# A seven-product matmul with three of its four results as one running sum in a PSUM bank

## The chip, the cores and the metric

The kernel runs on one core of a Trainium2 chip. The time is the device time of one execution in microseconds, as a median over runs; a profiled execution gives the span from the first to the last instruction, and the trace behind it. TensorE (PE) multiplies matrices, and its weight loads are listed as PEld; VectorE (DVE) and ScalarE (ACT) work elementwise; GpSimd (POOL) and SyncE (SP) mostly issue loads here.

## The reference

Two decoder layers over a sequence of 256 rows of width 2048, in float32. Per layer, cut to the matmuls that matter here:

```python
h = rmsnorm(x); proj = h @ w_in            # GLU pair, q, k, v, forget logits, two gates
y_conv = conv(...) @ w_conv_out;  y_attn = attention(...) @ w_attn_out
x = x + (sigmoid(g_conv) * y_conv + sigmoid(g_attn) * y_attn) @ w_out
gate, up = split(rmsnorm(x) @ w_gate_up)   # 2 x 5632 columns
x = x + (silu(gate) * up) @ w_down
x = x + sigmoid(rmsnorm(x) @ w_ple_gate) * (p[i] @ w_ple_proj)
```

A final rmsnorm ends it. Nearly all the work is a 256-row operand times a wide weight matrix that is read once.

## The kernel before, in words

**Precision and slabs.** A matmul here works on float32r numbers. To keep float32's precision each operand is split into a high part h and a rest l, and a product is three matmuls: xh wh, xh wl, xl wh (`Sum.add`, lines 181 to 186). A weight slab is a tile `raw` of 128 x 1024 (two k-blocks of 128 by 512 columns, 512 KB). `fetch` (133) loads it through SP's queue into one of 8 `raw` buffers. `split` (138) makes h by a ScalarE copy (line 141, the rounding) and l by a VectorE subtraction (line 142); five buffers each, `wh` and `wl`. Two k-blocks, two blocks of 128 rows and three matmuls make 12 matmuls of 512 columns a plain slab.

**The seven-product form.** `fast_chunks` (238) computes two column chunks of 512, weights w1 and w2, over all of k. Of the k-groups of 512 it takes the first one or two (`fast`) in a form with seven products instead of eight; the rest are plain slabs. For a fast group, A11 and A12 are the halves of w1's slab pair, "A21" = w2's first half and A22 = w2's second half; the operand's four blocks and four of their sums are kept in `Fast` (343), made by `make` (362) as M1, T2, T3, N4X. Each product has 6 matmuls. Results go to seven running sums: `c11`, `c12` and `c21` are parts of the result tiles c1 and c2 in the two-bank PSUM tiles `mm`; `p1`, `q5`, `q6`, `q7` have a bank `ms` each, which is all four of the `ms` banks. Transposes and small matmuls use `ms` banks too.

**Order in a group** (lines 274 to 292). Fetch a11 and sm (w2's first half); POOL's queue adds w1's first half onto sm while it loads (276). Fetch a22 and a12. Products: p1 with a11, c21 with a22, a plain slab (`go`), c11 with a12, usually another plain slab, q7 with sm; then VectorE adds a22 to sm; q6 with it; a11 becomes sm - a11; q5; a12 becomes a12 + sm; c12. The three VectorE sums work in place on raw tiles (helpers in lines 271 and 272).

**Evacuation** (lines 293 to 297, 300, 304). ScalarE copies p1 to `u1`; VectorE takes q6 from it, adds q7, and adds q5 twice: four instructions of 128 x 512 that read a bank. After more plain slabs c1 is added to u1, and c2 minus u2 is the second result. Other work (transposes, attention steps, the depthwise convolution on VectorE) is put between the plain slabs after the evacuation, by the queues `turns`, `tasks` and `background`.

**What sets the order.** Each engine runs its queue in order. The framework that builds the queues follows the program's order as a priority: it may put a later instruction ahead of one whose inputs would not be there yet. Semaphores and buffers are its work too: a load waits until its buffer is free, and a write into a bank waits for readers of what was there.

**Where it is called.** `fast_chunks` runs 48 times: the two gates, the output projection, gate/up, down, and the per-layer embedding gate.

Of the kernel before, what the change touches and what calls it, by code (L numbers as in the profile page):

```python
# [12 lines left out]
AF = mybir.ActivationFunctionType  # L13
ALU = mybir.AluOpType
# [31 lines left out]
def trunk(ctx, tc, xT, xR, pT, wI, wF, wC, wA, wOut, wGU, wD, wPG, wPP, vec, bF, gF, out):  # L46
    nc = tc.nc
# [11 lines left out]
    act, dve, pe = nc.scalar, nc.vector, nc.tensor  # L59
    uid = iter(range(1 << 30))  # L60

    def pair(dtype=F32):
        return pairs.tile([P, 2, 512], dtype, tag="pair", name=f"pair{next(uid)}")
# [20 lines left out]
    def run():  # L84
        for _ in range(len(turns)):
            turns.popleft()()
        if tasks:
            tasks.popleft()()

    def fill(n):  # L90
        credit[0] += n
        while background and credit[0] > 0:
            cost, op = background.popleft()
            credit[0] -= cost
            op()
        if not background:
            credit[0] = 0
# [35 lines left out]
    def fetch(src):  # L133
        raw = raws.tile([P, 2, 512], F32, tag="raw", name=f"raw{next(uid)}")
        nc.sync.dma_start(raw.rearrange("p k n -> p (k n)"), src)
        return raw

    def split(raw):
        h = whs.tile([P, 2, 512], F32R, tag="wh", name=f"wh{next(uid)}")
        l = wls.tile([P, 2, 512], F32R, tag="wl", name=f"wl{next(uid)}")  # L140
        act.activation(h, raw, AF.Copy)  # L141
        dve.tensor_tensor(l, raw, h.bitcast(F32), op=ALU.subtract)  # L142
        recent[0] = h
        return h, l
# [26 lines left out]


    class Sum:
        def __init__(self, n, bank):
            self.n, self.left, self.bank = n, n, bank

        @property
        def t(self):
# [2 lines left out]
        def add(self, xh, xl, wh, wl):  # L181
            start = self.left == self.n
            self.left -= 1
            pe.matmul(self.t, lhsT=xh, rhs=wh, start=start, stop=False)  # L184
            pe.matmul(self.t, lhsT=xh, rhs=wl, start=False, stop=False)  # L185
            pe.matmul(self.t, lhsT=xl, rhs=wh, start=False, stop=self.left == 0)  # L186

    def once(make):

        made = []  # L190

        def get():
            if not made:
                made.append(make())
            return made[0]

        return get

    def sums_of_blocks(n1, n2=None):
        t = once(bank_mm)  # L200
        return t, Sum(n1, lambda: t()[:, 0, :]), Sum(n1 if n2 is None else n2, lambda: t()[:, 1, :])

    def plain(sums, xs, k0, parts, blocks=range(2)):
        h, l = parts
        for kk in range(2):
            for b in blocks:
                xh, xl = xs[k0 + kk]
                sums[b].add(xh(b), xl(b), h[:, kk, :], l[:, kk, :])

    def await_x(xs, ks):  # L210
        while not all(k in xs for k in ks):
            assert turns or tasks
            run()
# [24 lines left out]
    def fast_chunks(fast, w1, w2, xs, ks, first, by_block=None):  # L238

        nf, nk = 2 * len(fast), 4 * len(ks)
        p1, q5, q6, q7 = (Sum(nf, once(bank_ms)) for _ in range(4))
        c1, c11, c12 = sums_of_blocks(nf + nk)
        c2, c21, c22 = sums_of_blocks(nf + nk, nk)
        if by_block is not None:
            c22 = Sum(nk, once(bank_ms))
        left = deque()
        for w, sums in ((w1, (c11, c12)), (w2, (c21, c22))):
            for g, k0 in enumerate(ks):  # L250
                for half in range(2):
                    left.append((w[len(fast) + g][:, half * 1024 : (half + 1) * 1024], sums, k0 + 2 * half))
        state = dict(quiet=True)

        def go(n=1):
            for _ in range(n):
                src, sums, k0 = left.popleft()
                parts = split(fetch(src))
                await_x(xs, (k0, k0 + 1))
                plain(sums, xs, k0, parts)  # L260
                if not state["quiet"]:
                    fill(CONV // 2 + len(left) % 2)
                    run()

        def product(to, operand, raw):
            h, l = split(raw)
            xh, xl = operand
            for kk in range(2):
                to.add(xh(kk), xl(kk), h[:, kk, :], l[:, kk, :])

        add = lambda o, a, b: dve.tensor_tensor(o, a, b, op=ALU.add)  # L271
        sub = lambda o, a, b: dve.tensor_tensor(o, a, b, op=ALU.subtract)  # L272
        u1, u2 = pair(), pair()
        for g, f in enumerate(fast):
            a11, sm = fetch(w1[g][:, :1024]), fetch(w2[g][:, :1024])
            nc.gpsimd.dma_start(sm.rearrange("p k n -> p (k n)"), w1[g][:, :1024], accum_op=ALU.add)
            a22, a12 = fetch(w2[g][:, 1024:]), fetch(w1[g][:, 1024:])
            product(p1, f(B11), a11)
            product(c21, f(N4X), a22)
            go()  # L280
            product(c11, f(B21), a12)
            if len(left) > 2 * len(ks):
                go()
            if nk == 8 and len(fast) == 1:
                run()
            product(q7, f(T3), sm)
            add(sm, sm, a22)
            product(q6, f(T2), sm)
            sub(a11, sm, a11)
            product(q5, f(M1), a11)  # L290
            add(a12, a12, sm)
            product(c12, f(B22), a12)
        act.activation(u1[:, 0, :], p1.t, AF.Copy)
        sub(u1[:, 1, :], u1[:, 0, :], q6.t)
        add(u2[:, 0, :], u1[:, 1, :], q7.t)
        add(u1[:, 1, :], u1[:, 1, :], q5.t)
        add(u2[:, 1, :], u2[:, 0, :], q5.t)
        state["quiet"] = False
        go(len(left) - 2 * len(ks))
        add(u1, u1, c1())  # L300
        first(u1)
        if by_block is None:
            go(len(left))
            sub(u2, c2(), u2)
            return u2
        go(len(left) - 4)
        held = [(split(fetch(src)), k0) for src, _, k0 in left]
        for b, c in enumerate((c21, c22)):
            for parts, k0 in held:
                plain([c, c], xs, k0, parts, [b])  # L310
            sub(u2[:, b, :], c.t, u2[:, b, :])
            by_block(b, u2)
# [25 lines left out]

        return (lambda b: o[:, b * P : (b + 1) * P]), (lambda b: o[:, S + b * P : S + (b + 1) * P])

    B11, B12, B21, B22, M1, T2, T3, N4X = range(8)

    class Fast:

# [17 lines left out]
        def make(self):  # L362
            f = lambda n: self.f[n // 4][:, n % 4]
            sub = lambda o, a, b, op: dve.tensor_tensor(f(o), f(a), f(b), op=op)  # L364
            sub(M1, B11, B12, ALU.subtract)
            sub(T2, M1, B22, ALU.add)
            sub(T3, B22, B12, ALU.subtract)
            sub(N4X, B21, T2, ALU.subtract)
            self.h, self.l = [], []
            for t in self.f:  # L370
                h, l = (pair(F32R).rearrange("p a b -> p (a b)") for _ in range(2))
                t = t.rearrange("p n k s -> p (n k s)")
                act.activation(h, t, AF.Copy)  # L373
                dve.tensor_tensor(l, t, h.bitcast(F32), op=ALU.subtract)  # L374
                self.h.append(h.rearrange("p (n k s) -> p n k s", n=4, k=2))
                self.l.append(l.rearrange("p (n k s) -> p n k s", n=4, k=2))
            self.f = None
# [167 lines left out]
    for i in range(L):  # L545
# [296 lines left out]
        def sigmoids(c, nf):  # L842

            ts = []

            def gate(t):
                for b in range(2):
                    act.activation(t[:, b, :], t[:, b, :], AF.Sigmoid, scale=norm.r(b))
                ts.append(t)

            gate(fast_chunks(norm.fast[:nf], wI[i, c], wI[i, c + 1], norm.xs, range(4 * nf, KD, 4), gate))
            return ts
# [38 lines left out]
        for n in range(0, N4, 2):  # L891
            by = (0, 1, 2, 3) if n == 0 else (0, 3, 1, 2)
            onto_x(norm, n + 1)(
                fast_chunks(
                    [fast_merged[g] for g in by[: 1 + n // 2]], *([wOut[i, m][g] for g in by] for m in (n, n + 1)),
                    merged, [4 * g for g in by[1 + n // 2 :]], onto_x(norm, n),
                )
            )
# [4 lines left out]
        for part, nch in enumerate(FFN_PARTS):  # L903
            hid = {}
            fast_hid = [Fast() for _ in range(nch - 2)]
            for c in range(c0, c0 + nch):
                w1, w2 = wGU[i, 2 * c], wGU[i, 2 * c + 1]
# [12 lines left out]
                else:  # L920
                    nf = 1 if c == c0 else 2
# [9 lines left out]
            for n in range(0, N4, 2):  # L931
                await_x(hid, (4 * c0,))
                on = after if part == len(FFN_PARTS) - 1 else None
                nf = 1 if n == 0 else len(fast_hid)
# [132 lines left out]
```

## Time and profile before

| | |
|---|---|
| median of 3 runs | 2793.24 us (2793.18 to 2793.36) |
| profiled execution | 2793.7 us, span 2791.8 us |
| granted TensorE clock | 0.999 |
| bytes read from HBM | 580.85 MB, 209 GB/s over the span |
| ACT busy | 1660.0 us, 59% |
| POOL busy | 79.4 us, 3% |
| DMA engines | 5 to 7 tenths busy in most slices |

How to read it: a group's row gives the line, the engine, the operation, out<-in by the program's names, shapes, the count, then busy time and the mean of one in ns, and behind the second bar the idle time before it and who ended it. Matmuls are pipelined: a record of 0.39 us overlaps its neighbours, and the distance between two starts is what one costs. In the view by windows a row is a stretch, its length, and then the busy time of each engine with its number of instructions, the clock, the DMA share and GB/s. A timeline row has start, duration, engine, line, operation, tiles, count, and in brackets the idle time before it with its releaser.

### The profile page before, as it was taken

To read this page: it belongs to the slowest core of one execution; us is meant where nothing else is said; L and a number is where in the kernel's file an instruction comes from. 1 tells how busy PE (TensorE), PEld (TensorE's weight loads), DVE (VectorE), ACT (ScalarE), POOL (GpSimd) and SP (SyncE) were. 2 spreads that over 40 slices of the span, in tenths; PEclk is the share of its full clock that TensorE was granted. 3 is DMA by queue.
4 is the path that set the end of the run, shared out by engine and by line. 5 is a ranking of instruction groups with operands and counts; after the bars stand their busy time and mean duration, and the time that the engine had idled before them with its cause. 6 is when DMAs were issued, how large, how long until landed. Compare 5 with 4: busy or idle time off the path is not lost.

```text
span 2791.8 us, 34941 instructions
## 1 busy us (share of the span) xinstructions
PE 2773.9 (99%) x12568; PEld 2293.5 (82%) x12568; DVE 2507.1 (90%) x3003; ACT 1660.0 (59%) x2002; POOL 79.4 (3%) x121
## 2 busy tenths in 40 slices
PE   9999999999999999999999999999999999999998
PEld 7888888888888888888888888888888888888886
DVE  7999889888989988999979988988799899889998
ACT  7445766565556655656754466655665565556565
POOL 0000000000000000000000000000000000000000
PEclk9999999999999999999999999999999999999999
DMA  7555557666676766776655555575666677677674
GB/s 299 188 182 185 199 186 227 198 217 201 217 226 220 227 218 220 224 221 203 215 186 190 185 181 199 189 233 184 228 205 215 216 232 231 203 229 218 217 239 131
DMA packets 161597, 585.24 MB, mean 210 GB/s; under 512 B 18192, under 2 KB 18448, under 8 KB 161168
## 3 DMA queue, kind: packets, MB, share of 16 engines
q1 hardware_dynamic: 149040, 539.50, 56.5%
q0 software_dynamic: 11520, 41.95, 8.3%
q8 instruction: 98, 1.61, 0.2%
q10 hardware_dynamic: 864, 1.57, 0.2%
q14 instruction: 75, 0.61, 0.1%
HBM read 580.85 MB, written 2.10 MB: 209 GB/s over the span
## 4 chain that ended last, share of the span: by engine, by line
PE 93%; DVE 3%; issue 3%; ACT 1%; POOL 0%; POOLq 0%; ACTq 0%; DVEq 0%
PE mm L186 25%; PE mm L185 25%; PE mm L184 25%; PE ms L184 5%; PE ms L185 5%; PE ms L186 5%; PE ms L334 2%; DVE wl L142 1%; DVE raw L271 0%; PE ms L726 0%; ACT wh L141 0%; PE ms L755 0%; DVE pair L374 0%; PE ms L745 0%; DVE pair L271 0%
## 5 line engine op out<-in xcount | busy, mean ns | idle before, releaser
L141 ACT ACTIVATE wh<-raw 128x1024 fp32r<-128x1024 f32 x1254 | 1300.5, 1058 | 1022.7 <-PE mm L186 576.7
L142 DVE TENSOR_TENSOR wl<-raw,wh 128x1024 fp32r<-128x1024 f32 x1254 | 1501.0, 1219 | 212.4 <-ACT wh L141 204.9
L184 PE MATMUL mm<-wh,pair 128*128 128x512 f32 x3224 | 1261.9, 392 | 1.1 <-ACT pair L324 0.7
L185 PE MATMUL mm<-wl,pair 128*128 128x512 f32 x3224 | 1256.6, 390 | 0.9 <-DVE wl L142 0.8
L186 PE MATMUL mm<-wh,pair 128*128 128x512 f32 x3224 | 1256.8, 390 | 0.5 <-DVE pair L325 0.5
L186 PEld LDWEIGHTS mm<-wh,pair 128*128 128x128 f32 x3224 | 605.2, 188 | 128.4 <-DVE pair L325 1.4
L185 PEld LDWEIGHTS mm<-wl,pair 128*128 128x128 f32 x3224 | 605.6, 188 | 126.3 <-DVE wl L142 3.2
L184 PEld LDWEIGHTS mm<-wh,pair 128*128 128x128 f32 x3224 | 605.4, 188 | 126.0 <-ACT pair L324 1.7
L184 PE MATMUL ms<-wh,pair 128*128 128x512 f32 x680 | 265.7, 391 | 0.1
L186 PE MATMUL ms<-wh,pair 128*128 128x512 f32 x680 | 264.7, 389 | 0.0
L185 PE MATMUL ms<-wl,pair 128*128 128x512 f32 x680 | 264.6, 389 | 0.0
L569 DVE SCALAR_TENSOR_TENSOR pair<-pair,vecs,pair 128x256 f32<-128x256 f32 x480 | 201.1, 474 | 0.0
L271 DVE TENSOR_TENSOR raw<-raw,raw 128x1024 f32<-128x1024 f32 x160 | 195.4, 1222 | 2.6
L184 PEld LDWEIGHTS ms<-wh,pair 128*128 128x128 f32 x680 | 127.7, 188 | 28.0 <-ACT pair L998 0.9
L186 PEld LDWEIGHTS ms<-wh,pair 128*128 128x128 f32 x680 | 127.6, 188 | 26.7
L185 PEld LDWEIGHTS ms<-wl,pair 128*128 128x128 f32 x680 | 127.7, 188 | 26.0
L272 DVE TENSOR_TENSOR raw<-raw,raw 128x1024 f32<-128x1024 f32 x80 | 98.0, 1225 | 2.6
L271 DVE TENSOR_TENSOR pair<-pair,ms 128x512 f32<-128x512 f32 x144 | 93.9, 680 | 0.0
L272 DVE TENSOR_TENSOR pair<-mm,pair 128x1024 f32<-128x1024 f32 (+1 forms) x48 | 58.1, 1210 | 11.5 <-PE mm L186 11.4
L271 DVE TENSOR_TENSOR pair<-pair,mm 128x1024 f32<-128x1024 f32 x48 | 58.3, 1215 | 5.5 <-PE mm L186 5.5
L374 DVE TENSOR_TENSOR pair<-pair,pair 128x1024 fp32r<-128x1024 f32 x52 | 62.8, 1217 | 0.0
L373 ACT ACTIVATE pair<-pair 128x1024 fp32r<-128x1024 f32 x52 | 54.3, 1055 | 2.7 <-DVE pair L364 1.6
(168 smaller groups left out, 1065.0 us busy)
## 6 DMA issues: line engine op xcount, KB each, us to landing
raw<-in_wGU_dram SPq DMA_DIRECT2D x352, 512.0 KB, 4.8
raw<-in_wI_dram SPq DMA_DIRECT2D x287, 512.0 KB, 4.0
raw<-in_wD_dram SPq DMA_DIRECT2D x176, 512.0 KB, 4.8
raw<-in_wOut_dram SPq DMA_DIRECT2D x64, 512.0 KB, 4.6
raw<-in_wPG_dram SPq DMA_DIRECT2D x64, 512.0 KB, 4.9
raw<-in_wGU_dram POOLq DMA_DIRECT2D x36, 512.0 KB, 7.9
raw<-in_wA_dram SPq DMA_DIRECT2D x32, 512.0 KB, 4.7
raw<-in_wC_dram SPq DMA_DIRECT2D x32, 512.0 KB, 4.9
```

Of the source, the lines that this page charges most:

```text
L141: act.activation(h, raw, AF.Copy)
L142: dve.tensor_tensor(l, raw, h.bitcast(F32), op=ALU.subtract)
L184: pe.matmul(self.t, lhsT=xh, rhs=wh, start=start, stop=False)
L185: pe.matmul(self.t, lhsT=xh, rhs=wl, start=False, stop=False)
L186: pe.matmul(self.t, lhsT=xl, rhs=wh, start=False, stop=self.left == 0)
L271: add = lambda o, a, b: dve.tensor_tensor(o, a, b, op=ALU.add)
L272: sub = lambda o, a, b: dve.tensor_tensor(o, a, b, op=ALU.subtract)
L334: pe.transpose(pt[:, kk * S + b * P : kk * S + (b + 1) * P], src(b)[:, c : c + P], ident)
L373: act.activation(h, t, AF.Copy)
L374: dve.tensor_tensor(l, t, h.bitcast(F32), op=ALU.subtract)
L569: dve.scalar_tensor_tensor(cv[c], u[c][:, j : j + S], w, cv[c], op0=ALU.mult, op1=ALU.add,)
```

## The change

p1, q6 and q7 become one running sum `chain` in one bank with three stations: after the products with B11 it holds p1; after those with NT2 (the negative of T2) it holds p1 - q6; after those with T3 it holds p1 - q6 + q7. ScalarE copies it at each station. `Sum` gets an argument `rests`, so that the last matmul of each third is marked as an end. The products with a11 of all groups go to the start of the call, those with sm (T3) to its end; sm is fetched first and each later group's sm ahead of the sums of the group before; the sum sm + a22 is put into a22 instead of sm. `u1` and `u2` are taken from their pool later. In `make`, T2 becomes NT2 by one scalar_tensor_tensor instruction.

```diff
     class Sum:
-        def __init__(self, n, bank):
-            self.n, self.left, self.bank = n, n, bank
+        def __init__(self, n, bank, rests=1):
+            self.n, self.left, self.bank, self.rest = n, n, bank, n // rests
...
-            pe.matmul(self.t, lhsT=xl, rhs=wh, start=False, stop=self.left == 0)
+            pe.matmul(self.t, lhsT=xl, rhs=wh, start=False, stop=self.left % self.rest == 0, **kw)
...
-        p1, q5, q6, q7 = (Sum(nf, once(bank_ms)) for _ in range(4))
+        chain, q5 = Sum(3 * nf, once(bank_ms), 3), Sum(nf, once(bank_ms))
...
-        u1, u2 = pair(), pair()
+        def third(g):
+            sm = fetch(w2[g][:, :1024])
+            nc.gpsimd.dma_start(sm.rearrange("p k n -> p (k n)"), w1[g][:, :1024], accum_op=ALU.add)
+            return sm
+
+        s3 = [third(0)]
+        a11s = []
         for g, f in enumerate(fast):
-            a11, sm = fetch(w1[g][:, :1024]), fetch(w2[g][:, :1024])
-            nc.gpsimd.dma_start(sm.rearrange("p k n -> p (k n)"), w1[g][:, :1024], accum_op=ALU.add)
+            a11s.append(fetch(w1[g][:, :1024]))
+            product(chain, f(B11), a11s[g])
+        u1 = pair()
+        act.activation(u1[:, 0, :], chain.t, AF.Copy)
+        for g, f in enumerate(fast):
+            a11, sm = a11s[g], s3[g]
             a22, a12 = fetch(w2[g][:, 1024:]), fetch(w1[g][:, 1024:])
-            product(p1, f(B11), a11)
             product(c21, f(N4X), a22)
             go()
             product(c11, f(B21), a12)
...
-            product(q7, f(T3), sm)
-            add(sm, sm, a22)
-            product(q6, f(T2), sm)
-            sub(a11, sm, a11)
+            if g < len(fast) - 1:
+                s3.append(third(g + 1))
+            add(a22, sm, a22)
+            product(chain, f(NT2), a22)
+            if g == len(fast) - 1:
+                act.activation(u1[:, 1, :], chain.t, AF.Copy)
+            sub(a11, a22, a11)
             product(q5, f(M1), a11)
-            add(a12, a12, sm)
+            add(a12, a12, a22)
             product(c12, f(B22), a12)
-        act.activation(u1[:, 0, :], p1.t, AF.Copy)
-        sub(u1[:, 1, :], u1[:, 0, :], q6.t)
-        add(u2[:, 0, :], u1[:, 1, :], q7.t)
+        for sm, f in zip(s3, fast):
+            product(chain, f(T3), sm)
         add(u1[:, 1, :], u1[:, 1, :], q5.t)
+        u2 = pair()
+        act.activation(u2[:, 0, :], chain.t, AF.Copy)
         add(u2[:, 1, :], u2[:, 0, :], q5.t)
...
-            sub(T2, M1, B22, ALU.add)
             sub(T3, B22, B12, ALU.subtract)
-            sub(N4X, B21, T2, ALU.subtract)
+            dve.scalar_tensor_tensor(f(NT2), f(M1), -1.0, f(B22), op0=ALU.mult, op1=ALU.subtract)
+            sub(N4X, B21, NT2, ALU.add)
```

More of the change, by code (lines that the diff above doesn't have):

```diff
@@ L183, in add @@
             self.left -= 1
-            pe.matmul(self.t, lhsT=xh, rhs=wh, start=start, stop=False)
-            pe.matmul(self.t, lhsT=xh, rhs=wl, start=False, stop=False)
-            pe.matmul(self.t, lhsT=xl, rhs=wh, start=False, stop=self.left == 0)
+            kw = dict(skip_group_check=self.rest < self.n)
+            pe.matmul(self.t, lhsT=xh, rhs=wh, start=start, stop=False, **kw)
+            pe.matmul(self.t, lhsT=xh, rhs=wl, start=False, stop=False, **kw)
+            pe.matmul(self.t, lhsT=xl, rhs=wh, start=False, stop=self.left % self.rest == 0, **kw)
     def once(make):
@@ L339, in by_blocks @@
         return (lambda b: o[:, b * P : (b + 1) * P]), (lambda b: o[:, S + b * P : S + (b + 1) * P])
-    B11, B12, B21, B22, M1, T2, T3, N4X = range(8)
+    B11, B12, B21, B22, M1, NT2, T3, N4X = range(8)
     class Fast:
```

## The prediction

> **What bounds the kernel now.** The page first: totals, chain and costliest groups.
>
> ```profile
> span 2791.8 us, 34941 instructions
> ...
> PE 2773.9 (99%) x12568; PEld 2293.5 (82%) x12568; DVE 2507.1 (90%) x3003; ACT 1660.0 (59%) x2002; POOL 79.4 (3%) x121
> ...
> PE 93%; DVE 3%; issue 3%; ACT 1%; POOL 0%; POOLq 0%; ACTq 0%; DVEq 0%
> ...
> L141 ACT ACTIVATE wh<-raw 128x1024 fp32r<-128x1024 f32 x1254 | 1300.5, 1058 | 1022.7 <-PE mm L186 576.7
> L142 DVE TENSOR_TENSOR wl<-raw,wh 128x1024 fp32r<-128x1024 f32 x1254 | 1501.0, 1219 | 212.4 <-ACT wh L141 204.9
> ...
> L569 DVE SCALAR_TENSOR_TENSOR pair<-pair,vecs,pair 128x256 f32<-128x256 f32 x480 | 201.1, 474 | 0.0
> ...
> L272 DVE TENSOR_TENSOR raw<-raw,raw 128x1024 f32<-128x1024 f32 x80 | 98.0, 1225 | 2.6
> L271 DVE TENSOR_TENSOR pair<-pair,ms 128x512 f32<-128x512 f32 x144 | 93.9, 680 | 0.0
> ```
>
> TensorE is busy for 99% of the span and holds 93% of the chain; VectorE is close behind with 90%. The profiled execution took 2793.7 us, 1.9 more than its span; the median of the three runs shown is 2793.24, so differences worked out on the span carry over as they are. L272's x80 counts groups: 48 calls (L271's 144 is three a call) hold 80 groups, of one or two each, so 32 calls have two groups and 16 have one.
>
> Where TensorE's 18 idle microseconds lie, the view by windows tells (columns: stretch, its length, then busy time of PE, PEld, DVE, ACT, POOL).
>
> ```profile
> 0.00:258.00 258.00, 254.88 (x1170) 209.92 (x1171) 232.35 (x435) 141.43 (x201) 5.38 (x26) 1.00 0.61 211
> 258.00:2756.00 2498.00, 2495.99 (x11299) 2064.88 (x11298) 2247.56 (x2533) 1503.13 (x1779) 72.34 (x93) 1.00 0.66 211
> 740.00:1270.00 530.00, 530.00 (x2374) 439.24 (x2374) 484.56 (x468) 310.10 (x332) 17.90 (x21) 1.00 0.70 221
> 1125.50:1167.20 41.70, 41.70 (x189) 34.59 (x189) 41.42 (x42) 27.13 (x29) 1.61 (x3) 1.00 0.72 226
> 2779.00:2792.00 13.00, 0.02 (x1) 0.00 (x0) 5.48 (x14) 4.27 (x9) 1.66 (x2) 0.68 0.43 161
> ```
>
> The seven-product calls fill the second row. TensorE idles 2.0 us of its 2498; the other 16 are the first 258 us and the 13 us behind the last matmul, where the change has nothing. One call of two groups is the fourth row: TensorE has no gap in 41.7 us, and VectorE only 0.3. Both are full, but the first sets the pace as long as VectorE delivers in time.
>
> **Matmuls.** The change issues the same products with as many matmuls each: three sums of 2 x groups steps become one of 6 x groups. TensorE's work changes by 0. So a gain can only come out of waits, and these are small:
>
> ```profile
> PEld mm L185 <- DVE wl L142: 3.2, 7, 0.9
> PEld ms L334 <- DVE xt L881: 2.2, 6, 0.8
> ```
>
> The view of waits (us in total, times, longest) gives TensorE's weight loads 3.2 us behind VectorE's splitting (L142). With the 2.0 idle, which overlap with it, the gain is bounded by about 5.2 us. Two banks come free, but no transpose (L334) waits for a bank in that view, so this is worth 0.
>
> **VectorE and ScalarE.** Lines from the view by line and form:
>
> ```profile
> L272 DVE TENSOR_TENSOR pair<-pair,ms 128x512 f32<-128x512 f32 x48 | 32.6, 680 | 0.0
> L293 ACT ACTIVATE pair<-ms 128x512 f32<-128x512 f32 x48 | 27.7, 578 | 0.0
> L364 DVE TENSOR_TENSOR pair<-pair,pair 128x256 f32<-128x256 f32 x52 | 21.7, 418 | 1.9 <-ACT pair L358 1.8
> ```
>
> Two of four 680 ns sums over a bank go: 48 x 1.36 = 65.3 us off VectorE. NT2 as a scalar_tensor_tensor is taken at L569's 474 instead of 418 ns, 26 times: 1.5 us back. VectorE falls to about 2443. ScalarE gets two more copies a call, 48 x 2 x 0.578 = 55.5 us, to about 1716; in the call above it is idle 14.6 of 41.7 us, which hides 1.2. Each is 0 on the path as long as TensorE has no gap; of the 5.2 us I take 0.6.
>
> **What the new order asks of VectorE.** I lay it over the same call, whose first product starts at 1125.55. First TensorE (start, duration), then VectorE.
>
> ```profile
> 1125.55 0.39 PE L184 MATMUL ms<-wh,pair 128*128 128x512 f32 x1
> 1135.07 0.39 PE L184 MATMUL ms<-wh,pair 128*128 128x512 f32 x1
> 1136.42 0.39 PE L184 MATMUL ms<-wh,pair 128*128 128x512 f32 x1
> 1138.01 0.39 PE L185 MATMUL ms<-wl,pair 128*128 128x512 f32 x1
> 1141.64 0.39 PE L186 MATMUL ms<-wh,pair 128*128 128x512 f32 x1
> ```
>
> ```profile
> 1129.92 1.21 DVE L142 TENSOR_TENSOR wl<-raw,wh 128x1024 fp32r<-128x1024 f32 x1
> 1131.16 1.23 DVE L271 TENSOR_TENSOR raw<-raw,raw 128x1024 f32<-128x1024 f32 x1
> 1132.42 1.23 DVE L272 TENSOR_TENSOR raw<-raw,raw 128x1024 f32<-128x1024 f32 x1
> 1133.58 1.23 DVE L142 TENSOR_TENSOR wl<-raw,wh 128x1024 fp32r<-128x1024 f32 x1
> 1134.72 1.22 DVE L271 TENSOR_TENSOR raw<-raw,raw 128x1024 f32<-128x1024 f32 x1
> 1135.86 9.33 DVE L142 TENSOR_TENSOR wl<-raw,wh 128x1024 fp32r<-128x1024 f32 x8
> ```
>
> The 42 matmuls from 1125.55 to 1135.07 give 0.227 us each: a product (6) takes 1.36 us, a plain slab (12) 2.72. Before, p1, c21, slab, c11, slab, q7 are 48 matmuls, and q6 starts at 1136.42. Afterwards two a11 products, c21, slab, c11, slab are 48 as well, so NT2 starts there too. Up to it VectorE makes six splits and three sums in either order, so its dates stay: NT2's split ends at 1134.81 (1.6 us early), q5's at 1135.86 + 1.2 = 1137.1 against the 1138.01 at which its second matmul reads it, 0.9 early. The two sums missing at the call before can add up to 1.36. In the second group five products follow each other (NT2, q5, c12, T3 twice) where there were four, but T3's splits need no sum before them, 1.2 us of VectorE for 1.36 of TensorE. Forecast: no gap opens, cost 0.
>
> **The wait that is new.** NT2's products may enter the bank only after the first copy, T3's only after the second. NT2 comes c21, slab, c11 and slab behind: 36 matmuls, 8.2 us. T3 comes q5 and c12 behind: 12, 2.72 us. How long a copy takes to get its turn, ScalarE shows behind p1, whose last matmul is the row at 1141.64:
>
> ```profile
> 1142.06 1.07 ACT L141 ACTIVATE wh<-raw 128x1024 fp32r<-128x1024 f32 x1 [0.20 <-PE ms L186]
> 1143.03 0.58 ACT L293 ACTIVATE pair<-ms 128x512 f32<-128x512 f32 x1
> ```
>
> That matmul ends at 1142.03. One rounding (L141), freed by the same matmul, goes ahead; the copy ends at 1143.61, 1.6 us after the product. T3 needs it within 2.72: 1.1 to spare, cost 0. Queued behind a waiting copy are the roundings of coming slabs, which lead VectorE. The other bound: two roundings more ahead make 1.6 + 2 x 1.06 = 3.7, a stop of 1.0 us a call, 48 us in all. I take 0, the nearer row.
>
> [...]
>
> **Loads.** There are 8 raw buffers. sm of each group is now held until T3 at the end of the call, a22 until a12's sum; the second group's a11 comes early. In SP's queue sm goes ahead of a11, on POOL the accumulating load follows it as before, and sm is first needed by the sum instead of by a split, no earlier: 0. But the third buffer to come free for the second group's loads was a22's, behind the sum that ended at 1132.39. Now a22 is free only behind NT2's split and a12's sum, at 1135.94:
>
> ```profile
> 1132.42 0.33 SPq L135 DMA_DIRECT2D raw<-in_wGU_dram  x1
> 1136.02 0.33 SPq L135 DMA_DIRECT2D raw<-in_wGU_dram  x1
> DMA to landing us min/median/max: 3.8/3.8/3.8
> raw<-in_wGU_dram SPq DMA_DIRECT2D x352, 512.0 KB, 4.8
> ```
>
> The third row is the landing of the 1136.02 load alone. The second group's first slab, which took the buffer at 1132.42, would be loaded by 1139.8, rounded by 1140.9, split by 1142.1. TensorE reaches it after NT2, q5, c12 and c21, at 1141.87, and reads the split 0.23 later, at 1142.1. Just in time; with the page's median of 4.8 it is 1.0 late, unless VectorE's 1.36 us relief has moved everything up. I take 0.
>
> Sum: 0 (matmuls) - 0.6 (waits) + 0 + 0 + 0; 2793.24 - 0.6 = 2792.6.
>
> **Rivals.** *The late buffer stops TensorE.* For it: a margin of 0 at 3.8 us and loads of 4.8 in the median. Against: the relief, and VectorE having nothing idle to lose. It decides when landing exceeds 3.8 plus what VectorE is ahead, 5.2 at most. Half a microsecond in each of the 32 calls gives 2793.2 + 16 = 2809; a whole one, 2825. *The copy comes late*, above: 2841; for it speaks only that ScalarE, with roundings of 1058 ns, has no free moment of its own for a copy in such a burst. *VectorE is the bound*: if TensorE's 99% were stretched records, the 64 us taken off VectorE would come out whole, 2729. Against it stand starts 0.227 apart through the call. [...]
>
> **How the numbers follow.** A measurement here tells 0.2% (5.6 us) from no change. Forecast (no new gap): 0.72. Late buffer 0.17 and late copy 0.06, both slower: 0.23. VectorE the bound: 0.05, the only way to be faster, since the 5.2 us bound lies under 5.6. The range goes from that bound, 2788, to the late buffer at half a microsecond, 2809; beyond lie the 0.05 and about half of the 0.23.
>
> **What would show it.** Right: L271's sums over ms fall to 96 and L272's go, copies become 144; VectorE near 2443, ScalarE near 1716; TensorE idle about 2 us in the calls' stretch. Late buffer: ScalarE's L141 waits for the landing of raw, and TensorE's gap is at the slab behind the second group's c21. Late copy: TensorE's ms waits for ScalarE's copy before T3. A span under 2786 would make the first argument wrong.

## The result, and the profile after

The changed kernel takes 2804.76 us (median of 5, 2802.63 to 2806.69) against 2793.18 for the kernel before (median of 5, 2792.53 to 2793.36): a ratio of 1.0043, 95% interval 1.0031 to 1.0055. It is slower by 11.6 us, where no change was forecast. The profiled execution took 2804.53 us, span 2802.8, which is 11.0 more than the span before.

The page of the changed kernel, the totals and the groups that the change touches (code lines have moved: matmuls L186 to L188, additions L273, subtractions L274):

```profile
span 2802.8 us, 35052 instructions
...
PE 2776.5 (99%) x12568; PEld 2294.7 (82%) x12568; DVE 2449.6 (87%) x2907; ACT 1707.5 (61%) x2098; POOL 78.8 (3%) x121
...
L186 PE MATMUL mm<-wh,pair 128*128 128x512 f32 x3224 | 1262.9, 392 | 8.0 <-DVE pair L274 7.8
...
L273 DVE TENSOR_TENSOR raw<-raw,raw 128x1024 f32<-128x1024 f32 x160 | 195.2, 1220 | 10.7 <-DMA raw<-in_wD_dram 8.7
...
L273 DVE TENSOR_TENSOR pair<-pair,ms 128x512 f32<-128x512 f32 x96 | 65.4, 681 | 10.0 <-PE ms L188 9.7
```

The busy totals are as forecast: as many matmuls, VectorE 57.5 us lighter, ScalarE 47.5 heavier. The loss stands behind the second bars: `mm` products waited 7.8 us for VectorE's L274 on a `pair` tile, and VectorE's sums on raw tiles waited 8.7 us for a load. Both rows show next to nothing in that place before.

The view by windows gives the stretch of the seven-product calls, as before (stretch, length, busy PE, PEld, DVE, ACT, POOL, clock, DMA share, GB/s):

```profile
258.00:2756.00 2498.00, 2486.52 (x11249) 2056.01 (x11248) 2178.58 (x2429) 1541.40 (x1865) 72.31 (x93) 1.00 0.66 210
```

TensorE started 50 matmuls fewer in the same time; at 0.227 us each that is 11.3 us, the whole loss. It idled 11.5 us instead of 2.0, 9.5 more; another 1.6 us are slower starts behind one of its stops (last section). The view of waits says for what (us in total, times, longest):

```profile
ACT wh L141 <- DMA raw<-in_wGU_dram: 41.8, 24, 3.1
ACT wh L141 <- DMA raw<-in_wI_dram: 17.8, 9, 4.6
ACT wh L141 <- DMA raw<-in_wD_dram: 14.8, 5, 4.5
...
DVE raw L273 <- DMA raw<-in_wD_dram: 8.7, 6, 1.9
PE mm L186 <- DVE pair L274: 7.8, 6, 2.2
...
PE mm L187 <- DVE wl L142: 2.7, 3, 1.6
...
PE ms L349 <- DVE xt L981: 1.3, 1, 1.3
```

TensorE stops six times, 7.8 us in all, for an evacuation of two banks by VectorE. The other two rows of TensorE, for splits and for the input of transposes, were 0.8 and 0.7 before, so 2.5 more. No row has TensorE waiting for a ScalarE copy of `chain`. ScalarE's roundings (L141) wait for loads 84.1 us in 44 places (with 5.2 and 4.5 for two other weights), where they waited 4.5 us in 2 places before.

One of the six stops, TensorE's timeline in the changed kernel at the start of a down call that follows a gate/up call:

```profile
1215.37 0.39 PE L188 MATMUL mm<-wh,pair 128*128 128x512 f32 x1
1217.87 0.60 PE L186 MATMUL mm<-wh,pair 128*128 128x512 f32 x1 [2.11 <-DVE pair L274]
1218.27 0.63 PE L187 MATMUL mm<-wl,pair 128*128 128x512 f32 x1
1218.70 0.63 PE L188 MATMUL mm<-wh,pair 128*128 128x512 f32 x1
```

VectorE's timeline, same kernel and place:

```profile
1210.69 1.23 DVE L273 TENSOR_TENSOR raw<-raw,raw 128x1024 f32<-128x1024 f32 x1 [1.94 <-DMA raw<-in_wD_dram]
1211.84 1.22 DVE L142 TENSOR_TENSOR wl<-raw,wh 128x1024 fp32r<-128x1024 f32 x1
1212.97 1.22 DVE L274 TENSOR_TENSOR raw<-raw,raw 128x1024 f32<-128x1024 f32 x1
1214.11 1.22 DVE L142 TENSOR_TENSOR wl<-raw,wh 128x1024 fp32r<-128x1024 f32 x1
1215.36 1.22 DVE L273 TENSOR_TENSOR raw<-raw,raw 128x1024 f32<-128x1024 f32 x1
1216.51 1.22 DVE L274 TENSOR_TENSOR pair<-mm,pair 128x1024 f32<-128x1024 f32 x1
```

The last row is the evacuation of c2 of the gate/up call; c2's last matmul ended near 1213.0. It runs 3.5 us later, because five instructions of the *next* call stand ahead of it, three of them sums, and the first of these held the engine idle for 1.94 us until its load had landed. TensorE's next c-sum needs the two banks and starts at 1217.87. The same place in VectorE's timeline of before:

```profile
1209.27 1.22 DVE L272 TENSOR_TENSOR pair<-mm,pair 128x1024 f32<-128x1024 f32 x1 [0.35 <-PE mm L186]
...
1214.12 1.23 DVE L271 TENSOR_TENSOR raw<-raw,raw 128x1024 f32<-128x1024 f32 x1
```

There VectorE was waiting for c2, evacuated it at once, and came to the first sum 4.9 us after. Counted over VectorE's rows, raw sums stand within 9 us ahead of a two-bank evacuation in 0 of 48 calls before and in 34 after.

What the sum waited for is POOL's accumulating load, in the changed kernel's POOL timeline and in the summary of that one instruction:

```profile
1200.36 0.84 POOL L277 DMA_DIRECT2D raw<-in_wD_dram  x1 [27.15 <-DVE wl L142]
```

```profile
DMA to landing us min/median/max: 10.2/10.2/10.2
```

1200.36 + 10.2 is 1210.6, and the sum starts 0.1 later. The same load in POOL's timeline of before, and its landing:

```profile
1197.17 0.84 POOL L276 DMA_DIRECT2D raw<-in_wD_dram  x1 [29.59 <-DMA raw<-in_wD_dram]
```

```profile
DMA to landing us min/median/max: 10.7/10.7/10.7
```

It landed at 1207.9 there, 1.4 us before the evacuation of c2 at 1209.27; in the changed kernel 2.4 us before c2's last matmul ended. So this load is no later than before; the sum that needs it has come earlier. All six stops are at down calls behind a gate/up call. Over these six the load lands 1.4 to 3.7 us before c2's end in the kernel before and 2.4 to 4.2 in the changed one; the first sum stood 4.9 us behind c2's end and now starts 2.3 to 4.1 ahead of it, as soon as its load is there.

### The profile page after: what moved, and what is told of

Same layout as the page of the kernel before. It is cut to its first block, busy times and chain, and to the rows that moved or that the text cites. A ratio compares the mean times of both kernels' runs of the same rounds, so it can differ in the third digit from the quotient of the medians.

```text
span 2802.8 us, 35052 instructions
## 1 busy us (share of the span) xinstructions
PE 2776.5 (99%) x12568; PEld 2294.7 (82%) x12568; DVE 2449.6 (87%) x2907; ACT 1707.5 (61%) x2098; POOL 78.8 (3%) x121
## 5 line engine op out<-in xcount | busy, mean ns | idle before, releaser
L141 ACT ACTIVATE wh<-raw 128x1024 fp32r<-128x1024 f32 x1254 | 1303.3, 1058 | 956.3 <-PE mm L188 588.9
L142 DVE TENSOR_TENSOR wl<-raw,wh 128x1024 fp32r<-128x1024 f32 x1254 | 1495.0, 1219 | 278.7 <-ACT wh L141 273.0
L186 PE MATMUL mm<-wh,pair 128*128 128x512 f32 x3224 | 1262.9, 392 | 8.0 <-DVE pair L274 7.8
L187 PE MATMUL mm<-wl,pair 128*128 128x512 f32 x3224 | 1258.0, 390 | 2.7 <-DVE wl L142 2.7
L188 PE MATMUL mm<-wh,pair 128*128 128x512 f32 x3224 | 1256.9, 390 | 0.5 <-DVE pair L340 0.4
L186 PEld LDWEIGHTS mm<-wh,pair 128*128 128x128 f32 x3224 | 605.8, 188 | 134.5 <-ACT wh L141 10.4
L188 PEld LDWEIGHTS mm<-wh,pair 128*128 128x128 f32 x3224 | 605.7, 188 | 128.3 <-DVE pair L340 1.0
L187 PEld LDWEIGHTS mm<-wl,pair 128*128 128x128 f32 x3224 | 606.0, 188 | 127.7 <-DVE wl L142 4.7
L186 PE MATMUL ms<-wh,pair 128*128 128x512 f32 x680 | 265.3, 390 | 0.0
L188 PE MATMUL ms<-wh,pair 128*128 128x512 f32 x680 | 264.7, 389 | 0.0
L187 PE MATMUL ms<-wl,pair 128*128 128x512 f32 x680 | 264.6, 389 | 0.0
L273 DVE TENSOR_TENSOR raw<-raw,raw 128x1024 f32<-128x1024 f32 x160 | 195.2, 1220 | 10.7 <-DMA raw<-in_wD_dram 8.7
L186 PEld LDWEIGHTS ms<-wh,pair 128*128 128x128 f32 x680 | 127.7, 188 | 27.2 <-ACT pair L1013 0.8
L188 PEld LDWEIGHTS ms<-wh,pair 128*128 128x128 f32 x680 | 127.6, 188 | 26.6
L187 PEld LDWEIGHTS ms<-wl,pair 128*128 128x128 f32 x680 | 127.7, 188 | 26.2
L274 DVE TENSOR_TENSOR raw<-raw,raw 128x1024 f32<-128x1024 f32 x80 | 97.6, 1220 | 1.0
L273 DVE TENSOR_TENSOR pair<-pair,ms 128x512 f32<-128x512 f32 x96 | 65.4, 681 | 10.0 <-PE ms L188 9.7
L273 DVE TENSOR_TENSOR pair<-pair,mm 128x1024 f32<-128x1024 f32 x48 | 58.3, 1215 | 6.4 <-PE mm L188 6.4
L274 DVE TENSOR_TENSOR pair<-mm,pair 128x1024 f32<-128x1024 f32 (+1 forms) x48 | 57.9, 1205 | 1.9 <-PE mm L188 1.8
```

Of the source, the lines that this page charges most:

```text
L186: pe.matmul(self.t, lhsT=xh, rhs=wh, start=start, stop=False, **kw)
L187: pe.matmul(self.t, lhsT=xh, rhs=wl, start=False, stop=False, **kw)
```

## The experiments

**The theory (queue).** Before, the first sum of a group read sm and wrote it, so it stood behind sm's split. Now S2 = sm + a22 goes into a22's tile and needs only a22's split and sm's load. The framework that fills the queues finds it ready early and puts it ahead of c2's evacuation of the call before. In the six rows above from 1210.69 on nothing overtook the waiting sum in VectorE's queue: c2 ended near 1213.0, and its evacuation started behind the five others, at 1216.51. So where sm's load has not landed at the sum's new place, c2's evacuation is late, and TensorE has no bank. **Rival one (bank):** the running sum in one bank and its copies cost the time. **Rival two (buffers):** sm, a22 and a11 are held longer, loads start later, and lateness itself costs, whatever the order of the queue. All ratios below are to the kernel before, measured beside each (medians 2792.5 to 2792.7).

### a_evac: only the order in VectorE's queue

The first sum of a call is ordered behind c2's evacuation of the call before; nothing else is changed.

```diff
-            add(a22, sm, a22)
+            s2 = add(a22, sm, a22)
+            if evac:
+                tc.add_manual_dep(s2.ins, evac.pop().name, mybir.DependencyInfo(mybir.DependencyClass.NoSync, mybir.DependencyReason.DATA), reason="evac")
...
-            sub(u2, c2(), u2)
+            evac[:] = [sub(u2, c2(), u2).ins]
```

> The changed kernel with one thing more: VectorE's first sum of a call (sm onto a22) is queued behind the evacuation of c2 of the call before; no wait is taken away. Theory (queue): in the changed kernel's trace TensorE stops six times, 8.7 us in all (2.3, 1.5, 2.3, 1.1, 1.0, 0.6), each ended by VectorE's evacuation of c2, which stands in VectorE's queue behind sums that wait for sm's accumulating load. With the order turned round those six stops go, and 2804.8 falls by 8 to 9 us, to about 2796; the three stops at the embedding gate of the first layer (4.1 us) stay. Rival (one bank): the copies and the shared bank cost the time; then nothing moves, 2804. Rival (buffers): the loads are late because sm is held longer, and VectorE's split comes late either way; then at most half of it goes, 2800 to 2804.

2794.42 us (2792.92 to 2796.21), 1.0006 [0.9998, 1.0015]: 10.3 us of the 11.6 are back. (The six stops are the 7.8 us of the view of waits; counted as excess from start to start they are the 8.7 of the expectation.) Waits in a_evac:

```profile
ACT wh L141 <- DMA raw<-in_wGU_dram: 31.5, 21, 2.5
...
PE mm L187 <- DVE wl L142: 3.3, 5, 1.6
...
PE ms L352 <- DVE xt L984: 1.2, 1, 1.2
```

No TensorE wait for L275's evacuation is left, and VectorE's timeline of a_evac has it back on the heels of c2:

```profile
1209.45 1.23 DVE L275 TENSOR_TENSOR pair<-mm,pair 128x1024 f32<-128x1024 f32 x1 [0.40 <-PE mm L188]
...
1213.07 1.22 DVE L274 TENSOR_TENSOR raw<-raw,raw 128x1024 f32<-128x1024 f32 x1
```

ScalarE's roundings wait for loads nearly as long as in the changed kernel (71.0 us in 45 places), and at eight buffers that alone costs little: TensorE's small waits of the changed kernel stay.

### a_keep: the sum as late as the program has it

```diff
-            add(a22, sm, a22)
+            tc.keep_in_program_order(add(a22, sm, a22))
```

> The changed kernel with the first sum of every group queued behind all of VectorE's work that stands before it in the program (splits of the slabs, evacuation of c2, what the call before left). Theory (queue): all nine long stops go, the three of the embedding gate too (VectorE's split behind a sum ends two of them), 2792 to 2795, unless the later sums make TensorE wait for NT2's split. Rival (one bank): 2804. Rival (buffers): 2800 to 2804.

2835.4 us (2833.89 to 2836.2), 1.0152 [1.0138, 1.0165]: a miss, 31 us slower than the change itself. Waits in a_keep:

```profile
PE ms L186 <- ACT wh L141: 8.6, 4, 3.9
PE mm L187 <- DVE wl L142: 8.0, 16, 0.8
PE ms L187 <- DVE wl L142: 6.0, 16, 0.6
```

Now every group's sum, not just a call's first, stands behind all earlier work, and the splits that feed NT2 and the slabs come late. The sum's place has a floor as well as a ceiling: early it blocks the evacuation, late it starves the products.

### a_banks: four banks again, in the new order

```diff
-        chain, q5 = Sum(3 * nf, once(bank_ms), 3), Sum(nf, once(bank_ms))
+        p1, q5, q6, q7 = (Sum(nf, once(bank_ms)) for _ in range(4))
...
+        act.activation(u1[:, 0, :], p1.t, AF.Copy)
+        add(u1[:, 1, :], u1[:, 0, :], q6.t)
+        add(u2[:, 0, :], u1[:, 1, :], q7.t)
```

> The changed kernel with p1, q5, q6 and q7 in four banks again and VectorE's evacuation as before (sums of 680 ns in place of ScalarE's two copies); the order of the loads, the products and the sums stays as changed. Theory (queue): order and holding are the cause, not the bank, so the six stops at c2's evacuation stay, and VectorE has 65 us more: 2803 to 2812. Rival (one bank): back to 2793. Rival (buffers): as the theory, 2803 to 2812; this run tells only the bank apart.

2808.6 us (2806.05 to 2812.29), 1.0056 [1.0043, 1.0069]. A loss at least as large is there without the running sum, so it does not need the bank or the copies, and rival one falls. But it is made of other stops, as a_banks's waits show:

```profile
PE mm L187 <- DVE wl L142: 5.6, 7, 1.6
...
PE mm L186 <- DVE pair L274: 3.2, 4, 1.1
```

The six stops did not stay, as the theory had it: there are four for the evacuation, with less than half the time, and more for splits. In the down calls three instructions stand ahead of the evacuation here, not five, and sums stand ahead of it in 24 calls, not 34. So the running sum has a part in how far ahead the sums are queued; whether by the bank, the copies or the work that it takes off VectorE was not tried.

### b_s2: the kernel before with S2 in the other tile

```diff
-            add(sm, sm, a22)
-            product(q6, f(T2), sm)
-            sub(a11, sm, a11)
+            add(a22, sm, a22)
+            product(q6, f(T2), a22)
+            sub(a11, a22, a11)
...
-            add(a12, a12, sm)
+            add(a12, a12, a22)
```

> The kernel before with one part of the change: the sum of sm and a22 goes into a22's tile instead of sm's. Four banks, S3's products in their old place, sm held no longer than before. Theory (queue): the sum no longer depends on sm's split, only on its load, so it may be queued ahead of c2's evacuation; if this part alone makes the stops, some of them show, 2796 to 2803. Rival (buffers): sm is not held until the call's end, so the loads come in time and nothing moves, 2793 to 2794. Rival (one bank): 2793.

2795.03 us (2793.89 to 2796.18), 1.0009 [1.0, 1.0018], between the two expectations. The turned order arises from this edit alone: sums stand ahead of the evacuation in 26 of 48 calls (0 before). But only two of them wait, in b_s2's waits:

```profile
DVE raw L271 <- DMA raw<-in_wD_dram: 1.4, 2, 1.0
```

No L141 rounding waits for a load here. In the six down calls three instructions stand ahead of the evacuation, where the changed kernel has five: the sum comes about 2.4 us before c2's end, and its load lands 1.8 to 3.8 us before it. Of TensorE's waits in this run 0.3 us is for the evacuation, and the longest, 1.5 us, is for one ScalarE rounding. So the turned order by itself costs next to nothing at the evacuation; the stops need a sum that is queued ahead of its load's landing as well. The queue theory as first stated was half of it. What puts five instructions ahead in the changed kernel, beyond the running sum (a_banks), was not tried alone.

### a_noacc: without the accumulating load

```diff
-            nc.gpsimd.dma_start(sm.rearrange("p k n -> p (k n)"), w1[g][:, :1024], accum_op=ALU.add)
```

> The changed kernel without the accumulating loads on POOL's queue: w1's first half is not added onto sm, so S3 is computed from w2's half alone; 42 MB less are loaded. The first sum then waits for sm's plain load alone. Theory (queue): the sum has nothing to wait for, c2's evacuation behind it is on time or nearly, the six stops go: 2794 to 2798. Rival (order alone): the stops stay, 2803 to 2805. Rival (one bank): 2803 to 2805.

2793.59 us (2792.05 to 2794.71), 1.0002 [0.9993, 1.0011]. The order is still turned in 34 calls, and ScalarE's roundings still wait 74.2 us for plain loads in 42 places, but sm is complete with its plain load, and of TensorE's six stops for the evacuation one is left:

```profile
PE mm L186 <- DVE pair L274: 0.8, 1, 0.8
```

The load that the sums waited for was POOL's, the second half of a chain of two loads into the same tile.

### a_r9p27 and b_r9p27: a ninth raw buffer

Both kernels with one raw buffer more, paid for by one `pair` buffer; nothing else.

```diff
-PAIRS = 28
+PAIRS = 27
...
-RAWS = 8
+RAWS = 9
```

> The changed kernel with nine raw buffers instead of eight (and 27 pair tiles instead of 28). Theory (queue): the six sums that wait 8.7 us for sm's accumulating load get it one load earlier; VectorE's order stays, so the six stops shrink to what the order alone costs, under 0.5 us each: 2795 to 2799. Rival (buffers alone): all loads come in time again, 2792 to 2794. Rival (order alone): the stops stay at 8 us, 2804.

> The kernel before with the same nine raw buffers and 27 pair tiles, to read the run above by. Only 3 of its 1016 loads come just when they are needed, so both theories expect no change: 2792 to 2794.

The changed kernel with nine buffers: 2790.38 us (2790.05 to 2791.15), 0.9992 [0.9983, 1.0001], lower than either expectation. The kernel before with nine: 2793.05 (2792.54 to 2793.49), 1.0001 [0.9992, 1.0010], as it was. The kernel before gains nothing from a ninth buffer. Waits, the calls' stretch by windows, and then VectorE's timeline in a_r9p27:

```profile
ACT wh L141 <- DMA raw<-in_wGU_dram: 5.0, 3, 1.7
...
PE mm L187 <- DVE wl L142: 2.6, 3, 1.6
```

```profile
258.00:2756.00 2498.00, 2495.65 (x11309) 2066.72 (x11308) 2191.72 (x2440) 1559.23 (x1873) 72.39 (x93) 1.00 0.66 211
```

```profile
1202.53 1.21 DVE L273 TENSOR_TENSOR raw<-raw,raw 128x1024 f32<-128x1024 f32 x1
...
1207.63 1.23 DVE L273 TENSOR_TENSOR raw<-raw,raw 128x1024 f32<-128x1024 f32 x1
1208.77 1.22 DVE L274 TENSOR_TENSOR pair<-mm,pair 128x1024 f32<-128x1024 f32 x1
```

The sums still run ahead of the evacuation (34 of 48 calls, five instructions in the six down calls), but without a wait before them: the first starts 5.4 us before c2's end, and its load has landed 6.8 to 7.8 us before it. The evacuation comes 0.8 us behind c2's end. This is the best kernel of the study: no execution of it overlaps with one of before, though 2.3 us is under the 0.2% that the prediction took for telling a difference, and the interval just reaches 1.

### a_best: the sum also behind the first split

a_evac, with the sum also ordered behind the split of its group's first slab (the helper `split` leaves its last instruction in `lastl`):

```diff
+            evac.append(lastl[0])
...
-            if evac:
+            while evac:
```

> The changed kernel with VectorE's first sum of a group queued behind two things: the evacuation of c2 of the call before, and the split of the group's first plain slab. With the first alone the time was 2794.4, with stops of 1.8, 0.8 and 1.4 us left at the first layer's embedding gate, two of them ended by VectorE's split (L142), which stands behind a sum and the embedding's product there. Theory (queue): the second edge takes the two stops at the split, 2.6 us: 2791 to 2793, about what the kernel before takes or one or two less. Rival (buffers): the slabs there are loaded late, so the order changes nothing, 2794.

2813.56 us (2812.75 to 2814.05), 1.0074 [1.006, 1.0088]: a miss. Waits in a_best:

```profile
PE mm L187 <- DVE wl L142: 8.2, 15, 1.2
```

As in a_keep, TensorE's stops are for splits where the sum is held back for longer than the evacuation needs. With eight buffers no order tried here beats the kernel before.

### a_banks_r9 and a_evac_r9: with nine buffers, what else is worth something

a_banks and a_evac, each with the edit of a_r9p27 on top.

> The changed kernel with four banks and VectorE's evacuation as before, order as changed, and nine raw buffers with 27 pair tiles: what the running sum in one bank is worth where the loads are on time. With nine buffers the changed kernel takes 2790.4 and the kernel before 2793.0. If the 65 us taken off VectorE bring the 2.6 us, this run takes 2793 to 2796; if the new order brings them, 2790.

> The changed kernel with both cures: the first sum queued behind c2's evacuation, and nine raw buffers with 27 pair tiles. Theory (queue): each cure takes the same six stops away, so together they bring no more than the better one, 2790 to 2791. Rival (order costs by itself): the sums stand ahead of c2's evacuation in 34 of 48 calls with nine buffers too; if that costs something in each, turning it round gains more, 2786 to 2789.

Four banks: 2793.89 us (2793.56 to 2794.51), 1.0004 [0.9995, 1.0013]. Against 2790.38 for a_r9p27 the running sum is worth 3.5 us with nine buffers, and no execution of one overlaps with one of the other; of the parts tried it is the only one that gains. The mended order: 2790.65 (2790.34 to 2791.29), 0.9993 [0.9984, 1.0001], the same as without it. The two cures are not additive, since each takes away one of two conditions:

| medians, us | sums ahead of the evacuation | evacuation first |
|---|---|---|
| 8 buffers: the load lands 2.3 to 4.2 us before c2's end | 2804.76 | 2794.42 |
| 9 buffers: it lands 5.4 to 7.8 us before c2's end | 2790.38 | 2790.65 |

### a_raws7 and b_raws7: a buffer fewer

RAWS = 7 in the changed kernel and in the one before.

> The changed kernel with seven raw buffers instead of eight. Theory (queue): the sums wait longer for sm's load with c2's evacuation behind them, and waits come in more calls: 2815 to 2860. Rival (bank or order alone): 2803 to 2806.

> The kernel before with seven raw buffers instead of eight: what a buffer less costs where no sum stands ahead of c2's evacuation. Theory (queue): loads come late, but only the splits wait and VectorE is ahead of TensorE: 2793 to 2800, less than half of what the changed kernel loses by its held buffers. Rival (buffers alone): a buffer less costs here what holding sm costs there, 2803 or more.

Changed: 2875.99 us (2870.51 to 2885.6, 4 runs), 1.0302 [1.0285, 1.0319], above what was expected, and mostly not by the expected stops: of TensorE's waits in a_raws7 27.1 us are for splits, 24.2 for ScalarE's roundings and 9.6 for the evacuation. Before: 2813.31 (2812.42 to 2814.08, 4 runs), 1.0074 [1.006, 1.0087]; here the queue theory's expectation missed and the buffers' was right. Waits in b_raws7:

```profile
ACT wh L141 <- DMA raw<-in_wGU_dram: 40.6, 31, 2.7
...
PE mm L184 <- DVE pair L272: 7.7, 8, 1.4
```

No raw sum stands ahead of an evacuation in this kernel, and yet TensorE waits for it 7.7 us. In VectorE's timeline of b_raws7 two splits with an operand sum of `make` (L374) between them stand right ahead of the evacuation at all eight of these stops; at one, c2's last matmul ends at 918.1 and the evacuation starts at 920.88. So what stands ahead of an evacuation need not be a raw sum, and with seven buffers late loads cost time whatever the order: rival two is right there, though not for the 11.6 us at eight. In buffers 9, 8, 7 the changed kernel reads 2790.4, 2804.8, 2876.0, the one before 2793.1, 2793.2, 2813.3: the times read as if the change had moved the kernel nearly one buffer down a curve on which it had been safe at eight, though the stops differ in kind.

## Why the prediction was wrong, point by point

**Right.** What bounds the kernel: TensorE at 0.227 us a start, the loss being 9.5 us more idle time of it and 1.6 us of slower starts (50 starts fewer, 11.3 us). Matmuls 0: x12568 as before. VectorE 2449.6 (forecast 2443): the two sums a call were priced at their record of 680 ns, but VectorE's next instruction starts 0.60 us behind such a sum (before, 1153.51 to 1154.11 and 1155.24 to 1155.84), and 96 x 0.60 makes 57.6, where 57.5 went and 65.3 was forecast. ScalarE 1707.5 (1716): the copies took 588 to 597 ns, not 578, but a record overlaps the next by about 0.1 us (1142.06 + 1.07 against 1143.03 in the prediction's rows), so 96 more added 47.5 to the busy total. Sums over `ms` 96; NT2 took 416 ns, not the 474 taken for it:

```profile
L382 DVE SCALAR_TENSOR_TENSOR pair<-pair,pair 128x256 f32<-128x256 f32 x26 | 10.8, 416 | 0.0
L286 ACT ACTIVATE pair<-ms 128x512 f32<-128x512 f32 x48 | 28.7, 597 | 10.9 <-PE ms L188 10.9
```

The new wait on the bank cost 0, as said: no TensorE row names these copies. The number of the bound, 5.2 us on any gain, holds (the best kernel gained 2.3), but by luck: it was added up from rows that did not shrink. In a_r9p27 weight loads wait 3.7 us for L142 (3.2 before) and TensorE idles 2.35 us in the calls' stretch (2.0 before). Yet 10 more matmuls start there than before, 2.3 us at 0.227; what shrank are other waits of weight loads, those for transposed inputs (xt) from 2.8 to 1.3 us and those for ScalarE's roundings from 2.0 to 0.2. Four banks were no faster than the change's one, 2793.89 against 2790.38 with nine buffers each; these two differ in VectorE's work as well, so they do not test the bank alone.

**The step that failed** is "Up to it VectorE makes six splits and three sums in either order, so its dates stay". The number of instructions stayed; their order did not. I laid the new program over the *old queue*, but the queue is made anew from dependences, and the change takes one away: the first sum no longer follows sm's split. It moved ahead of c2's evacuation of the call before, with the instructions behind it: from 4.9 us behind c2's end to 2.3 to 4.1 us ahead of it. So VectorE's dates did not stay, and a gap that was put at 0 took 7.8 us in six places.

**The step that hid it** is in the loads: "sm is first needed by the sum instead of by a split, no earlier: 0". By the program that is so; in VectorE's queue the sum came earlier than the split had been, in the place shown 1.94 us before its load had landed, though the load itself was no later than before. What stands behind a sum that waits for a load (c2's evacuation) and who waits for that (TensorE's banks) was not asked; that question, put to VectorE's queue at the *boundary between two calls* and not in the middle of one, would have found the place.

**The rivals.** The late buffer named the shortage rightly: a second group's first slab did come late, as ScalarE's timeline of the changed kernel has it in a gate/up call:

```profile
1184.75 2.01 ACT L141 ACTIVATE wh<-raw 128x1024 fp32r<-128x1024 f32 x2 [1.76 <-DMA raw<-in_wGU_dram]
```

But TensorE kept its 0.227 us through 1185 to 1192: in that place the lateness was covered. The six stops, 1.3 us each, lie in other places, where a sum waited for a load that was no later than before and an evacuation stood behind the sum. The price of 16 to 32 us was thus for the wrong place, and the 11.6 inside the range are not that rival's. The late copy and VectorE as the bound did not happen: 57.5 us less VectorE work gave nothing with eight buffers, and with nine the running sum that takes it off is worth 3.5.

**What stays open.** The 11.0 us of the profile are the 9.5 of idle time and the 1.6 of slower starts (below), 11.1 in all. The 9.5 are 7.8 (six stops) + 2.5 (more waits for splits and transposes), less about one in small waits of before that are gone. The 2.5 are left in a_evac too (rows of L187 and L352, 4.5 in all against 1.5 before). The wl part is left in a_r9p27 as well (2.6), so a shortage of buffers is not its cause; what is, was not tried alone.

## What to carry to other kernels

Where an edit changes which tile an instruction writes, it changes what that instruction depends on, and a framework that orders queues by readiness may move it across a stage's boundary (here in 34 of 48 calls): ask of every dependence that goes, what the instruction can now overtake, and whether what is overtaken gives back a bank. In VectorE's queue the sum that waited 1.94 us for its load held up what stood behind it, and the evacuation came 3.5 us after c2's end; with nine buffers, where the load had landed before the sum's place came, the same order cost nothing (2790.38 us, against 2790.65 with the evacuation first). So the place in the queue and the date of the landing must be judged together, and an earlier place can make late a load that is no slower than before (10.2 us from issue to landing, against 10.7). Of the cures, the one that brings the load forward (here a buffer) was safer than ordering by hand: of three orders tried, one helped (2794.42) and two made new stops (2813.56 and 2835.4).

## What the hardware showed that was not expected

One stop of 2.11 us cost more than itself. Behind it (1215.4 to 1217.9) TensorE's starts lie 0.427 us apart instead of 0.227, and the changed kernel's view by windows has the granted clock at 0.54 for 3.4 us:

```profile
1217.80:1221.20 3.40, 3.33 (x8) 2.65 (x9) 3.40 (x4) 0.00 (x0) 0.00 (x0) 0.54 0.39 143
```

That is 8 x 0.2 = 1.6 us more. The stop at 728.9 to 731.4, idle for 2.17 us, has no such tail; the granted clock is 1.00 from 731.4 to 735.0, and its third start is back at 0.22:

```profile
731.43 0.47 PE L186 MATMUL mm<-wh,pair 128*128 128x512 f32 x1 [2.17 <-DVE pair L274]
731.74 0.39 PE L187 MATMUL mm<-wl,pair 128*128 128x512 f32 x1
731.96 0.39 PE L188 MATMUL mm<-wh,pair 128*128 128x512 f32 x1
```

So of two stops of nearly the same length one had a tail and one had none, which may be why executions of the changed kernel spread over 4.1 us where those before spread over 0.8; that was not shown run by run. What decides between the two, no run here shows. In a_keep, whose longest stop is 3.9 us, the mean granted clock was 0.996 to 0.997, against 0.998 to 0.999 in the kernel before.

The accumulating load of 512 KB by POOL took 10.2 us to land at the place shown, the longest of the changed kernel's 80 (5.2 to 10.2, median 7.0). The plain loads of the same weight, in the changed kernel's page, have a median of 5.6:

```profile
raw<-in_wD_dram SPq DMA_DIRECT2D x176, 512.0 KB, 5.6
```
